# First stage of a hybrid backbone layer: fixed instruction order, squares paired and summed by TensorE, inverse norm multiplied in first

## Chip, cores and metric

The kernel runs on one NeuronCore of one Trainium2 chip. The metric is the time of the whole program on the device in microseconds; of several runs the median is given. All times inside a profile are microseconds from the first instruction of the profiled execution, unless they are marked ns.

## The reference, cut to what matters

One layer of a diffusion backbone over 1024 latent tokens and 256 context tokens, model width 1024. Both streams are normed, modulated (scale and shift made from a conditioning vector) and put through one wide projection; two recurrent branches, an output projection and a gated convolutional MLP follow.

```python
def rmsnorm(x, w):
    xf = x.astype(jnp.float32)
    y = xf * lax.rsqrt(jnp.mean(xf * xf, axis=-1, keepdims=True) + EPS)
    return (y * w.astype(jnp.float32)).astype(x.dtype)

def modulate(h, shift, scale):
    return h * (1 + scale) + shift
...
        mx = jnp.split((sc @ ada_w[l] + ada_b[l])[:, None, :], 6, axis=-1)
        mc = jnp.split((scc @ ada_w[l] + ada_b[l])[None, None, :], 6, axis=-1)
        hx = modulate(rmsnorm(x, norm_mix_w[l]), mx[0], mx[1])
        hc = modulate(rmsnorm(ctx, norm_mix_w[l]), mc[0], mc[1])
        oc, ox = mixer(hc, hx, w_in[l], ...
```

The change touches only the making of `hx` and `hc` and the first columns of the projection `h @ w_in`.

## The kernel before

Activations lie with the 1024 channels on partitions: eight tiles `xk[0..7]` of 128 channels x 1024 tokens for the latent stream, and `cx` (128 x 8 x 256) for the context. Every dense product is made in three passes on values split in two parts (`hi` = the value rounded to fp32r, `lo` = the rest): hi*hi, hi*lo, lo*hi. So each normed tile has a high and a low half (`xh[k]`, `xl[k]`, in the pool tiles H0 to H15; `ch[k]`, `cl[k]` for the context), and each weight tile a `whi` and a `wlo`, made by ScalarE and VectorE from the loaded `raw`.

`start()` is the first stage. SyncE's queue loads `xk`, `cx`, two groups of eight modulation weight tiles (`aw[0]` in H8 to H15, `aw[1]` in `adaw`), and the first weight tiles (`raw`: one for the step sizes, "dt", one for the recurrent input "lx", one for its gate "lg"). `norm_latent()` squares the eight `xk` on ScalarE and adds them up on VectorE into `ssx`; `token_rs()` sums over partitions by TensorE (line 199: a 128 x 128 block of the sums is the stationary operand, one column of ones the moving one; eight matmuls for 1024 tokens) and makes the inverse root (`rsqrt()`); `spread()` brings the result to all partitions (line 209: diagonal tiles `xdg` times ones, into PSUM), and ScalarE copies it to SBUF (`xrs`). `norm_context()` does the same for `cx`. `ada_group(q)` makes scale and shift (`sc`, `sv`) of four of the eight channel tiles: 32 matmuls at line 311, a copy `row`, two small matmuls at line 319, three VectorE instructions. Group 0 serves k = 0 to 3, group 1 serves k = 4 to 7.

Then a loop over k modulates one tile of each stream (`mod(k)`: value times scale times inverse norm on VectorE, `hi` with the shift on ScalarE, `lo` on VectorE) and hands four accumulations one step each (`gdense`, line 125): dt and lx over the context (`pre[0]`, `pre[1]`, 6 matmuls of 256 columns per k together), lx and lg over the latent tokens (`pre[2]`, `pre[3]`, 6 matmuls of 512 columns per k each). The last two lie in the pool `psD`, which has two buffers.

What order the instructions get on each engine is decided by the framework's scheduler: it may move an instruction ahead of others of its engine where the data allow it. `pin()` marks an instruction as kept in program order when `self.pinned` is set; before the change that is so only far later, in the MLP. Each engine, and SyncE's queue of transfers, works off its list strictly in that order.

Of the kernel before, what the change touches and what calls it, by code (L numbers as in the profile page):

```python
# [15 lines left out]
P = 128  # L16
# [29 lines left out]
class Builder:  # L46
# [31 lines left out]
    def wload(self, src, n=1024, kn=8):  # L78
        nc = self.nc
        with self.prio():  # L80
            raw = self.t(self.wp, n, "raw")
            nc.sync.dma_start(raw, src)
# [35 lines left out]
    def gdense(self, ps, w, xh, xl, spans, kn=8, xo=0):  # L118
        nc = self.nc
        hi, lo = w  # L120
        for k in range(kn):
            for i, (a, b) in enumerate(((hi, xh), (hi, xl), (lo, xh))):
                for (s, e) in spans:
                    o = ps[s // H] if isinstance(ps, list) else ps[:, s:e]
                    nc.tensor.matmul(o, a[:, k, :], b[k][:, xo + s : xo + e],  # L125
                                     start=(k == 0 and i == 0), stop=(k == kn - 1 and i == 2))
            yield
# [48 lines left out]
    def rsqrt(self, pool, ps, n, inv, tag):  # L176
# [5 lines left out]
        nc.vector.tensor_scalar(v, ps, inv, EPS, op0=ALU.mult, op1=ALU.add)  # L182
        self.act(a, v, AF.Sqrt)
        nc.vector.reciprocal(r, a)
        self.tt(a, r, r)
        self.tt(a, a, v)
        nc.vector.tensor_scalar(a, a, -0.5, 1.5, op0=ALU.mult, op1=ALU.add)
# [3 lines left out]
    def token_rs(self, pool, parts, n, inv, tag, ps=None):  # L191

        nc = self.nc
        nch = n // P
        if ps is None:
            ps = self.t(self.psS, nch, "s")
        for c in range(nch):
            for i, q in enumerate(parts):
                nc.tensor.matmul(ps[:, c : c + 1], q[:, c * P : (c + 1) * P], self.ones[:, 0:1],
                                 start=(i == 0), stop=(i == len(parts) - 1))  # L200
        return self.rsqrt(pool, ps[:, :nch], nch, inv, tag)

    def spread(self, pool, r, out, tag):

        nc = self.nc
        for c in range(r.shape[1]):
            dg = self.t(pool, P, tag + "dg")
            nc.vector.tensor_scalar(dg, self.ident, r[:, c : c + 1], None, op0=ALU.mult)
            nc.tensor.matmul(out[:, c * P : (c + 1) * P], self.ones, dg, start=True, stop=True)
# [61 lines left out]
    def setup(self, cpool):  # L271
# [14 lines left out]
        self.act(self.a_neg, self.v("a_log"), AF.Exp)  # L286
        nc.vector.tensor_scalar_mul(self.a_neg, self.a_neg, -1.0)
# [17 lines left out]
    def ada_group(self, pool, q, w, scc):  # L305
# [3 lines left out]
        for k in range(8):  # L309
            for g in range(4):  # L310
                nc.tensor.matmul(ps[32 * g : 32 * g + 32, :], scc[:, k, :], w[k][:, g * 256 : g * 256 + 256],
                                 start=(k == 0), stop=(k == 7))
# [5 lines left out]
        for i in range(2):  # L318
            nc.tensor.matmul(pt[:, i], row[:, i * P : (i + 1) * P], pick, start=True, stop=True)
# [32 lines left out]
    def start(self, cpool, ch, cl):  # L352
        nc, tc, A = self.nc, self.tc, self.A
        with tc.tile_pool(name="st1", bufs=1) as p1, tc.tile_pool(name="st2", bufs=2) as p2:
# [6 lines left out]
            for k in range(8):  # L361
                nc.sync.dma_start(aw[0][k], A["ada1"][0, k])
            scc = self.t(p1, [8, 32], "scc")
            nc.gpsimd.memset(scc, 0.0)
            self.lam_chain(cpool, p1)
            self.act(scc[:, :, 0:2], self.v("cc", n=16).rearrange("p (k i) -> p k i", i=2), AF.Silu)
            self.warm = self.t(cpool, 1, "warm")
            self.act(self.warm, self.ones[:, 0:1], AF.Sqrt)

            def norm_context():  # L370
                sq = [self.t(self.pH, [4, TX], f"H{h}") for h in range(2)]
                for h in range(2):
                    self.act(sq[h], cx[:, 4 * h : 4 * h + 4, :], AF.Square)
                self.tt(sq[0], sq[0], sq[1], op=ALU.add)
                self.tt(sq[0][:, 0:2], sq[0][:, 0:2], sq[0][:, 2:4], op=ALU.add)
                cr = self.token_rs(p1, [sq[0][:, 0], sq[0][:, 1]], TX, 1.0 / D, "cr")
                pcr = self.t(self.psS, TX, "s")
                self.spread(p2, cr, pcr, "x")
                crs = self.t(p1, TX, "ssc")
                self.act(crs, pcr, AF.Copy)  # L380
                return crs

            def norm_latent():
                ssx = self.t(p1, T, "ssx")
# [6 lines left out]
                pxr = [self.t(self.psS, H, "s") for _ in range(2)]  # L391
                xrs = self.t(p1, T, "ssx")
                for i in range(2):
                    self.spread(p2, xr[:, 4 * i : 4 * i + 4], pxr[i], "x")
                    self.act(xrs[:, i * H : i * H + H], pxr[i], AF.Copy)
                return xrs

            xrs = norm_latent()
            crs = norm_context()
            self.xh, self.xl = [], []  # L400

            def mod(k):
                self.modulate(cx[:, k, :], cx[:, k, :], crs, ch[k], cl[k], self.sc[:, k, 1:2], self.sv[:, k, 1:2])
# [4 lines left out]
            order = [("dt", -1), ("lx", M_LX), ("lg", M_LG)]  # L408
            self.wahead = 0
            ws = [self.take(key) for key in order[:2]]  # L410
            for k in range(8):
                nc.sync.dma_start(aw[1][k], A["ada1"][1, k])
            ws.append(self.take(order[2]))
            groups = [self.ada_group(p2, q, aw[q], scc) for q in range(2)]
            for _ in groups[0]:
                pass
            self.wahead = self.AHEAD[0]
            self.pre = [self.t(self.psS, TX, "s"), self.t(self.psS, TX, "s"),
                        self.t(self.psD, T, "d"), self.t(self.psD, T, "d")]
            X = [(0, TX)]  # L420
            gens = [self.gdense(self.pre[0], ws[0], ch, cl, X), self.gdense(self.pre[1], ws[1], ch, cl, X),
                    self.gdense(self.pre[2], ws[1], self.xh, self.xl, self.FULL),
                    self.gdense(self.pre[3], ws[2], self.xh, self.xl, self.FULL)]
# [1102 lines left out]
```

## Time and profile before

| | |
|---|---|
| median of 3 runs (lowest, highest) | 2298.85 us (2298.83, 2303.24) |
| the profiled execution's own time | 2300.16 us |
| its span, first to last instruction | 2298.4 us |
| TensorE busy | 2216.4 us, 96% |
| VectorE, ScalarE, GpSimd busy | 1627.4, 1178.3, 330.5 us |
| granted TensorE clock, mean over the span | 0.992 |
| last matmul of `start()` ends (line 125 on `pre[3]`) | 79.41 us |

The profiled execution's own time is 1.76 us more than its span, and 1.31 us above the median of the runs. A view called timeline lists instructions in order of time: start, length, engine, line, what it writes and reads, how many were merged (x4), and in brackets the idle time before it and what ended that. A view called windows gives each engine's busy time in a stretch. The profile shows a TensorE instruction as two records, PEld (load of the stationary operand) and PE (the matmul); a plain f32 matmul, as in the norms, is run as two such pairs.

### The profile page before, as it was taken

What the parts mean: (1) busy time and instruction counts of PE and PEld (TensorE: products, weight loads), DVE (VectorE), ACT (ScalarE), POOL (GpSimd) and SP (SyncE); (2) the same over time, 40 slices, a digit from 0 to 9 for tenths busy, and PEclk for the clock granted to TensorE, in tenths of its full rate; (3) what the DMA queues carried; (4) which work ended last, traced back from release to release, by engine and by line L of the source; (5) the groups of instructions that cost most, each with busy time, mean ns of one, the idle gap of its engine ahead of it and who ended that gap; (6) DMA issues with size and microseconds to landing.
All of it is one profiled execution on the core that took longest, in us unless ns stands there. A gap on an engine that the chain in (4) does not pass through costs nothing.

```text
span 2298.4 us, 29736 instructions
## 1 busy us (share of the span) xinstructions
PE 2216.4 (96%) x11302; PEld 1844.5 (80%) x11302; DVE 1627.4 (71%) x2554; ACT 1178.3 (51%) x1796; POOL 330.5 (14%) x255
## 2 busy tenths in 40 slices
PE   5999999999999999999999999999889999999998
PEld 3887888787888888888888778888668888878888
DVE  5789688889888858858866675457877777774335
ACT  4597888486666556656635322335334444442121
POOL 0000000000000000000000000001757777730000
PEclk9999999999999999999999999999999999999999
DMA  7222222243444434424348775532122222254212
GB/s 279 78 78 88 83 85 65 79 147 123 120 137 139 125 100 145 146 79 151 118 121 273 232 237 178 177 123 64 37 64 83 83 83 83 82 168 129 71 55 74
DMA packets 88943, 274.87 MB, mean 120 GB/s; under 512 B 10560, under 2 KB 16736, under 8 KB 84576
## 3 DMA queue, kind: packets, MB, share of 16 engines
q1 hardware_dynamic: 88800, 272.97, 37.2%
q8 instruction: 89, 1.46, 0.3%
q14 instruction: 54, 0.44, 0.1%
HBM read 233.85 MB, written 39.08 MB: 119 GB/s over the span
## 4 chain that ended last, share of the span: by engine, by line
PE 72%; DVE 11%; ACT 7%; DMA 6%; issue 3%; POOL 1%; SPq 0%; POOLq 0%; DVEq 0%; ACTq 0%
PE d L125 29%; PE s L125 17%; PE d L1173 11%; PE s L1173 5%; PE s L939 2%; ACT L L163 2%; ACT L163 2%; DMA adar<-in_ada 2%; PE s L931 1%; PE s L604 1%; DMA gk<-gd 1%; DVE wlo L160 1%; PE s L880 1%; DVE facc L157 1%; PE s L879 1%
## 5 line engine op out<-in xcount | busy, mean ns | idle before, releaser
L125 PE MATMUL d<-H,whi 128*128 128x512 f32 x2496 | 700.0, 398 | 2.9 <-ACT whi L163 1.6
L125 PEld LDWEIGHTS d<-H,whi 128*128 128x128 f32 x2496 | 456.4, 189 | 97.4 <-issue 5.6
L125 PE MATMUL d<-H,wlo 128*128 128x512 f32 x1248 | 392.3, 393 | 2.6 <-DVE wlo L160 2.6
L163 ACT ACTIVATE whi<-raw 128x1024 fp32r<-128x1024 f32 (+2 forms) x194 | 186.1, 960 | 290.1 <-PE s L125 117.1
L125 PEld LDWEIGHTS d<-H,wlo 128*128 128x128 f32 x1248 | 233.1, 188 | 52.5 <-DVE wlo L160 4.0
L157 DVE SCALAR_TENSOR_TENSOR facc<-d,vec,facc 128x945 f32<-128x945 f32 (+2 forms) x176 | 214.6, 1221 | 74.7 <-ACT facc L163 70.5
L160 DVE TENSOR_TENSOR wlo<-raw,whi 128x1024 fp32r<-128x1024 f32 (+1 forms) x154 | 188.0, 1222 | 76.8 <-ACT whi L163 70.1
L125 PE MATMUL s<-H,whi 128*128 128x512 f32 x672 | 202.6, 390 | 0.8 <-ACT whi L163 0.8
L163 ACT ACT_TABLE_LOAD x125 | 160.4, 1283 | 70.4 <-DVE bc L157 22.8
L1086 POOL TENSOR_TENSOR ssq<-H,A 128x512 f32<-128x512 f32 x4 | 6.0, 1501 | 1171.1 <-ACT H L163 1166.8
L125 PEld LDWEIGHTS s<-H,whi 128*128 128x128 f32 x672 | 125.7, 188 | 28.1 <-ACT whi L163 1.8
L125 PE MATMUL s<-A,whi 128*128 128x512 f32 x480 | 138.4, 390 | 1.1 <-POOL A L1086 1.0
L157 DVE SCALAR_TENSOR_TENSOR M<-s,mods,M 128x512 f32<-128x512 f32 (+1 forms) x72 | 49.5, 690 | 119.1 <-PE s L125 118.9
L125 PE MATMUL s<-H,wlo 128*128 128x512 f32 x336 | 126.0, 391 | 2.2 <-DVE wlo L160 2.1
L125 PEld LDWEIGHTS s<-A,whi 128*128 128x128 f32 x480 | 90.0, 188 | 20.6 <-POOL A L1086 1.4
L157 DVE SCALAR_TENSOR_TENSOR E<-E,cst 128x128 f32<-128x128 f32 x256 | 81.7, 350 | 22.6 <-ACT E L163 22.6
L160 DVE TENSOR_TENSOR L<-L,L 128x1280 f32<-128x1280 f32 (+3 forms) x50 | 69.7, 1401 | 38.8 <-ACT L L163 38.5
L163 ACT ACTIVATE m<-GU,dtt 128x128 f32<-128x128 f32 x256 | 79.1, 391 | 31.5 <-PE s L931 26.4
L1173 PE MATMUL d<-A,whi 128*128 128x512 f32 x372 | 91.6, 396 | 1.5 <-DVE facc L157 1.5
L157 DVE SCALAR_TENSOR_TENSOR m<-GL,dtt,m 128x128 f32<-128x128 f32 x256 | 78.2, 349 | 20.3 <-ACT m L163 20.3
L163 ACT ACTIVATE E<-E,cst 128x128 f32<-128x128 f32 x256 | 81.2, 393 | 21.0 <-DMA E<-csd 21.0
L1173 PE MATMUL d<-A,wlo 128*128 128x512 f32 x348 | 86.2, 398 | 5.2 <-ACT ssq L163 5.2
(333 smaller groups left out, 4250.3 us busy)
## 6 DMA issues: line engine op xcount, KB each, us to landing
raw<-in_w SPq DMA_DIRECT2D x92, 512.0 KB, 3.6
E<-csd SPq DMA_DIRECT2D x32, 1024.0 KB, 5.3
A<-in_wup SPq DMA_DIRECT2D x40, 512.0 KB, 4.2
R<-csd SPq DMA_DIRECT2D x64, 256.0 KB, 4.3
adar<-in_ada SPq DMA_DIRECT2D x32, 512.0 KB, 4.4
hd<-facc SPq DMA_DIRECT2D x22, 512.0 KB, 5.1
gated<-sg SPq DMA_DIRECT2D x32, 256.0 KB, 2.9
gd<-y SPq DMA_DIRECT2D x32, 256.0 KB, 3.6
```

What stands on the lines that cost most here:

```text
L125: nc.tensor.matmul(o, a[:, k, :], b[k][:, xo + s : xo + e], start=(k == 0 and i == 0), stop=(k == kn - 1 and i == 2))
L157: self.pin(self.nc.vector.scalar_tensor_tensor(out, in0, s, in1, op0=op0, op1=op1))
L160: return self.pin(self.nc.vector.tensor_tensor(out, a, b, op=op))
L163: return self.pin(self.nc.scalar.activation(out, in_, f, **kw))
L604: nc.tensor.matmul(pg, a[:, q, :], b[:, s:e], start=(i == 0), stop=(i == 2))
L879: nc.tensor.matmul(ps[:, s - s2, 0, :], btok[:, s, :], xw[:, 0, s, :], start=True, stop=True)
L880: nc.tensor.matmul(ps[:, s - s2, 1, :], btok[:, 7 - s, :], xw[:, 1, 7 - s, :], start=True, stop=True)
L931: nc.tensor.matmul(psy[q, c, :], self.xt[:, c0 + c, q], m[:, h, c, :], start=True, stop=True)
L939: nc.tensor.matmul(pso[:, c, :], S[:, cc if d == 0 else 7 - cc, d, :], CT[:, cc * P : (cc + 1) * P], start=True, stop=True)
L1086: self.pin(self.nc.gpsimd.tensor_tensor(out, a, b, op=op))
L1173: q = self.pin(self.nc.tensor.matmul(ps, a[:, k, :], b, start=(k == 0 and i == 0 and p in ("11", "12", "s3")), stop=(k == 3 and i == 2), s ...
```

## The change

It does five things, all inside `start()`:

- From the loads on, every instruction is pinned: each engine gets them in the order in which the code writes them.
- Squares are added in pairs (four VectorE adds instead of seven), and `token_sums()` lets TensorE add the four pair sums while it sums over partitions: 32 line-199 matmuls instead of eight.
- The inverse norm is not copied to SBUF. It stays in PSUM (`pxr`, one of `psD`'s two buffers) and is multiplied into `xk` and `cx` (`scaled(k)`, two halves per tile; two instructions for `cx`) ahead of scale and shift, which then need one ScalarE instruction per latent tile and one VectorE instruction per context tile; `hi` is a further ScalarE copy, `lo` a VectorE subtraction.
- `aw[1]` and the third weight tile (into H7) are asked for early in the code.
- Group 1 of the modulation is computed at k = 3 in one piece. The fourth accumulation starts after k = 5 and then makes up its first six steps at once, because its PSUM buffer is `pxr`'s until `scaled(7)`.

```diff
+            px = self.t(self.psS, 8, "s")
+            pairs = []
+            for k in range(KD):
+                sq = self.t(self.pH, T, f"H{k}" if k < 6 else "H6") if k != 7 else self.t(p1, T, "sq7")
+                self.act(sq, xk[k], AF.Square)
+                pairs.append(sq)
+                if k % 2:
+                    self.tt(pairs[k - 1], pairs[k - 1], sq, op=ALU.add)
...
-                for k in range(KD):
-                    s2 = ssx if k == 0 else self.t(p2, T, "modt")
-                    self.act(s2, xk[k], AF.Square)
-                    if k:
-                        self.tt(ssx, ssx, s2, op=ALU.add)
-                xr = self.token_rs(p1, [ssx], T, 1.0 / D, "xr")
...
+            self.token_sums(px, pairs[::2], 8)
+            xr = self.rsqrt(p1, px, 8, 1.0 / D, "xr")
+            self.tt(sq[0], sq[0], sq[1], op=ALU.add)
+            pxr = self.t(self.psD, T, "d")
+            self.spread(p2, xr, pxr, "x")
+            self.tt(sq[0][:, 0:2], sq[0][:, 0:2], sq[0][:, 2:4], op=ALU.add)
+            pc = self.t(self.psS, 2, "s")
+            self.token_sums(pc, [sq[0][:, 0], sq[0][:, 1]], 2)
+
+            def scaled(k):
+                for (s, e) in self.FULL:
+                    self.tt(xk[k][:, s:e], xk[k][:, s:e], pxr[:, s:e])
+
+            scaled(0)
+            cr = self.rsqrt(p1, pc, 2, 1.0 / D, "cr")
+            pcr = self.t(self.psS, TX, "s")
+            self.spread(p2, cr, pcr, "x")
+            scaled(1)
+            for h in range(2):
+                c = cx[:, 4 * h : 4 * h + 4, :]
+                self.tt(c, c, pcr.unsqueeze(1).to_broadcast([P, 4, TX]))
+            groups = [self.ada_group(p2, q, aw[q], scc) for q in range(2)]
+            next(groups[0])
+            next(groups[0])
...
+            def ctx(k):
+                self.pin(nc.vector.tensor_scalar(cx[:, k, :], cx[:, k, :], self.sc[:, k, 1:2], self.sv[:, k, 1:2],
+                                                 op0=ALU.mult, op1=ALU.add))
+                self.act(ch[k], cx[:, k, :], AF.Copy)
+
+            def latent(k):
                 self.xh.append(self.t(self.pH, T, f"H{2 * k}", F32R))
                 self.xl.append(self.t(self.pH, T, f"H{2 * k + 1}", F32R))
-                self.modulate(xk[k], xk[k], xrs, self.xh[k], self.xl[k], self.sc[:, k, 0:1], self.sv[:, k, 0:1])
+                self.act(xk[k], xk[k], AF.Identity, bias=self.sv[:, k, 0:1], scale=self.sc[:, k, 0:1])
+                self.act(self.xh[k], xk[k], AF.Copy)
+
+            def low(k):
+                self.tt(cl[k], cx[:, k, :], ch[k].bitcast(F32), op=ALU.subtract)
+                self.tt(self.xl[k], xk[k], self.xh[k].bitcast(F32), op=ALU.subtract)
...
             for k in range(KD):
-                mod(k)
-                if k in (1, 2):
-                    next(groups[1])
+                if k + 2 < KD:
+                    scaled(k + 2)
+                if k == 3:
+                    for _ in groups[1]:
+                        pass
+                if k + 1 < KD:
+                    ctx(k + 1)
+                    latent(k + 1)
+                low(k)
+                if k == 0:
+                    ws.append(self.wload(None, raw=raws[2]))
                 for g in gens:
                     next(g)
+                if k == 5:
+                    self.pre[3] = self.t(self.psD, T, "d")
+                    gens.append(self.gdense(self.pre[3], ws[2], self.xh, self.xl, self.FULL))
+                    for _ in range(6):
+                        next(gens[3])
+            self.pinned = False
+            self.wnext = 3
```

The other lines of the diff wrap existing instructions in `pin()`, give `wload` an already loaded `raw`, and split `token_sums` out of `token_rs`.

How the order on the engines moves is seen at three places. The first is TensorE's list at its very beginning, before: `ssx` holds the sum of all squares, and the eight matmuls of the latent sum stand as one row ahead of the spread and the context's sum.

```order
L199 MATMUL s_214<-ones_75,ssx_191 128x1 x8
L209 MATMUL s_233<-xdg_236,ones_75 128x128
L209 MATMUL s_233<-xdg_239,ones_75 128x128
L209 MATMUL s_233<-xdg_242,ones_75 128x128
L209 MATMUL s_233<-xdg_245,ones_75 128x128
```

Now, the last of eight token blocks and what follows it (H_66, H_68, H_70 and H_72 are the four pair sums):

```order
L204 MATMUL s_204<-ones_75,H_66_205 128x1
L204 MATMUL s_204<-ones_75,H_68_210 128x1
L204 MATMUL s_204<-ones_75,H_70_215 128x1
L204 MATMUL s_204<-ones_75,H_72_220 128x1
L213 MATMUL d_273<-xdg_274,ones_75 128x128
```

These four rows stand there eight times over, and since the first token block already needs the last pair sum, only three of the 32 matmuls stand ahead of the first one that does.

The second place is TensorE's list in the loop, before: `s_359` and `s_360` are the context accumulations, `d_361` the one of lx, `adaw` the weights of modulation group 1.

```order
L125 MATMUL s_359<-ch_12_97,whi_96_294 128x256
L125 MATMUL s_360<-ch_12_97,whi_99_300 128x256
L311 MATMUL s_397<-adaw_145,scc_161 32x256 x4
L125 MATMUL d_361<-H_111_366,whi_99_300 128x512 x2
L125 MATMUL s_359<-cl_20_105,whi_96_294 128x256
L125 MATMUL s_359<-ch_12_97,wlo_97_295 128x256
L125 MATMUL s_360<-cl_20_105,whi_99_300 128x256
L125 MATMUL s_360<-ch_12_97,wlo_100_301 128x256
L311 MATMUL s_397<-adaw_146,scc_161 32x256 x4
```

Now, around the end of k = 2 and the beginning of group 1 (`s_457`), with `d_374` the accumulation of lx:

```order
L126 MATMUL d_374<-H_111_415,whi_105_381 128x512 x2
L126 MATMUL d_374<-H_112_416,whi_105_381 128x512 x2
L126 MATMUL d_374<-H_111_415,wlo_106_382 128x512 x2
L313 MATMUL s_457<-adaw_143,scc_173 32x256 x4
L313 MATMUL s_457<-adaw_144,scc_173 32x256 x4
L313 MATMUL s_457<-adaw_145,scc_173 32x256 x4
L313 MATMUL s_457<-adaw_146,scc_173 32x256 x4
```

Group 1 stood between the first four steps of the loop, one weight tile at a time from the first step on; now all of it stands behind the third step's last matmul.

The third place is VectorE's list behind the scale and shift of group 0, before: the two `wlo` follow each other, and every `H` written is the low half of a latent tile.

```order
L160 TENSOR_TENSOR sv_79<-s_353,vec_72 128x8 x2
L157 SCALAR_TENSOR_TENSOR sc_80<-sv_79,vec_72 128x8
L157 SCALAR_TENSOR_TENSOR cx_119<-cx_119,sc_80,ssc_290 128x256
L157 SCALAR_TENSOR_TENSOR xk_29_120<-xk_29_120,sc_80,ssx_235 128x1024
L160 TENSOR_TENSOR wlo_97_295<-raw_292,whi_96_294 128x1024
L160 TENSOR_TENSOR wlo_100_301<-raw_298,whi_99_300 128x1024
L157 SCALAR_TENSOR_TENSOR cl_20_105<-cx_119,sv_79,ch_12_97 128x256
L157 SCALAR_TENSOR_TENSOR H_112_367<-xk_29_120,sv_79,H_111_366 128x1024
```

Now (`d_273` is `pxr`):

```order
L161 TENSOR_TENSOR sv_79<-s_362,vec_72 128x8 x2
L158 SCALAR_TENSOR_TENSOR sc_80<-sv_79,vec_72 128x8
L161 TENSOR_TENSOR wlo_99_369<-raw_159,whi_98_368 128x1024
L422 TENSOR_SCALAR cx_117<-cx_117,sc_80,sv_79 128x256
L161 TENSOR_TENSOR wlo_106_382<-raw_161,whi_105_381 128x1024
L161 TENSOR_TENSOR xk_31_120<-xk_31_120,d_273 128x512 x2
L422 TENSOR_SCALAR cx_117<-cx_117,sc_80,sv_79 128x256
L161 TENSOR_TENSOR cl_20_103<-cx_117,ch_12_95 128x256
L161 TENSOR_TENSOR H_104_378<-xk_29_118,H_103_377 128x1024
L161 TENSOR_TENSOR wlo_110_396<-H_55_163,whi_109_395 128x1024
```

The first `wlo` moved ahead of the context tile, the second one and `wlo_110` stand alone, each behind a `whi` that ScalarE makes after a whole latent tile. From the first matmul behind `start()` on, the lists of TensorE, VectorE and GpSimd are the same as before; on ScalarE and VectorE one split of a small weight tile (`gh`, `gl`) and in SyncE's queue one transfer (`gw`) stand earlier by a few places.

## Rows read from the trace of the kernel before

**Rows 1.** The page, its head and busy times of the whole span.
```profile
span 2298.4 us, 29736 instructions
...
PE 2216.4 (96%) x11302; PEld 1844.5 (80%) x11302; DVE 1627.4 (71%) x2554; ACT 1178.3 (51%) x1796; POOL 330.5 (14%) x255
```

**Rows 2.** Windows: stretch, length, PE, PEld, DVE, ACT, POOL busy, clock, DMA, GB/s.
```profile
17.90:40.80 22.90, 16.26 (x112) 12.67 (x112) 7.82 (x29) 5.78 (x11) 0.00 (x0) 1.00 0.96 381
40.80:79.40 38.60, 36.94 (x214) 26.43 (x215) 30.92 (x41) 17.92 (x23) 0.50 (x3) 0.96 0.18 53
79.40:260.00 180.60, 174.95 (x986) 151.13 (x985) 149.33 (x180) 149.23 (x184) 0.00 (x0) 1.00 0.27 84
```

**Rows 3.** Timeline of TensorE, 0 to 41 us.
```profile
17.92 3.55 PE L199 MATMUL s<-ones,ssx 128*128 128x1 f32 x16 [17.92 <-DVE ssx L160]
23.40 3.79 PE L209 MATMUL s<-xdg,ones 128*128 128x128 f32 x16 [1.94 <-DVE xdg L208]
27.72 1.87 PE L199 MATMUL s<-ones,H 128*128 128x1 f32 x8 [0.53 <-DVE H L160]
...
32.60 5.36 PE L311 MATMUL s<-H,scc 128*32 128x256 f32 x64
...
40.81 0.39 PE L125 MATMUL s<-ch,whi 128*128 128x256 f32 x1 [1.67 <-ACT ch L163]
```

**Rows 4.** Timeline of TensorE, 73 to 79.5 us.
```profile
73.04 1.09 PE L125 MATMUL d<-H,whi 128*128 128x512 f32 x4
...
75.78 0.28 PE L125 MATMUL s<-ch,whi 128*128 128x256 f32 x1
75.90 0.28 PE L125 MATMUL s<-cl,whi 128*128 128x256 f32 x1
...
78.79 0.62 PE L125 MATMUL d<-H,wlo 128*128 128x512 f32 x2
```

**Rows 5.** Timeline of SyncE's queue, 14 to 18 us (issues of transfers).
```profile
14.79 0.33 SPq L362 DMA_DIRECT2D H<-in_ada  x1
17.28 0.33 SPq L362 DMA_DIRECT2D H<-in_ada  x1
```

**Rows 6.** Groups by shape, 0 to 77 us: busy us, mean ns of one.
```profile
L163 ACT ACTIVATE H<-xk,sv 128x1024 fp32r<-128x1024 f32 x8 | 9.2, 1152 | 4.3 <-DVE xk L157 4.3
...
L163 ACT ACTIVATE whi<-raw 128x1024 fp32r<-128x1024 f32 x4 | 4.2, 1046 | 0.0
...
L157 DVE SCALAR_TENSOR_TENSOR cl<-cx,sv,ch 128x256 fp32r<-128x256 f32 x8 | 3.9, 485 | 0.0
```

**Rows 7.** Timeline of VectorE, 23 to 44 us.
```profile
23.06 0.88 DVE L208 TENSOR_SCALAR xdg<-ident,xrr 128x128 f32<-128x128 f32 x4
...
39.46 0.17 DVE L157 SCALAR_TENSOR_TENSOR sc<-sv,vec 128x8 f32<-128x8 f32 x1
...
41.40 2.36 DVE L160 TENSOR_TENSOR wlo<-raw,whi 128x1024 fp32r<-128x1024 f32 x2
```

**Rows 8.** Line 199 alone: ns min/median/max, first and last start in us.
```profile
L199 PE MATMUL s<-ones,ssx x16: 344/352/353, 17.9 to 21.1; 128*128 128x1 f32 x16
```

**Rows 9.** Timeline of TensorE at 644 us, the same instruction amid dense matmuls.
```profile
643.82 0.95 PE L199 MATMUL s<-ones,ssq 128*128 128x1 f32 x8
```

**Rows 10.** Groups by shape on VectorE, 76 to 260 us.
```profile
L214 DVE TENSOR_SCALAR L<-L 128x256 f32<-128x256 f32 x1 | 0.3, 295 | 0.5 <-ACT L L163 0.5
```

**Rows 11.** Instructions on the tile t: a 512-column product read from PSUM.
```profile
L160 DVE TENSOR_TENSOR t<-s,R x64: 681/691/694, 499.4 to 1193.9; 128x512 f32<-128x512 f32 x64
```

**Rows 12.** Instructions on adaw, group 1: ns min/median/max, first and last start.
```profile
L311 PE MATMUL s<-adaw,scc x64: 379/403/636, 42.1 to 56.0; 128*32 128x256 f32 x64
```

**Rows 13.** Windows: group 0's beginning, and a stretch early in the loop (columns as before).
```profile
32.60:35.90 3.30, 3.30 (x33) 1.58 (x36) 0.00 (x0) 0.39 (x1) 0.00 (x0) 1.00 1.02 408
42.80:46.20 3.40, 3.14 (x14) 1.55 (x14) 3.40 (x5) 0.43 (x1) 0.00 (x0) 0.52 0.70 200
```

**Rows 14.** The page's transfers: KB each, median us from issue to landing.
```profile
raw<-in_w SPq DMA_DIRECT2D x92, 512.0 KB, 3.6
```

More of the change, by code (lines that the diff above doesn't have):

```diff
@@ L124, in gdense @@
                     o = ps[s // H] if isinstance(ps, list) else ps[:, s:e]
-                    nc.tensor.matmul(o, a[:, k, :], b[k][:, xo + s : xo + e],
-                                     start=(k == 0 and i == 0), stop=(k == kn - 1 and i == 2))
+                    self.pin(nc.tensor.matmul(o, a[:, k, :], b[k][:, xo + s : xo + e],
+                                              start=(k == 0 and i == 0), stop=(k == kn - 1 and i == 2)))
             yield
@@ L207, in spread @@
             dg = self.t(pool, P, tag + "dg")
-            nc.vector.tensor_scalar(dg, self.ident, r[:, c : c + 1], None, op0=ALU.mult)
-            nc.tensor.matmul(out[:, c * P : (c + 1) * P], self.ones, dg, start=True, stop=True)
+            self.pin(nc.vector.tensor_scalar(dg, self.ident, r[:, c : c + 1], None, op0=ALU.mult))
+            self.pin(nc.tensor.matmul(out[:, c * P : (c + 1) * P], self.ones, dg, start=True, stop=True))
     def log1p01(self, e, d, s, q):
@@ L310, in ada_group @@
             for g in range(4):
-                nc.tensor.matmul(ps[32 * g : 32 * g + 32, :], scc[:, k, :], w[k][:, g * 256 : g * 256 + 256],
-                                 start=(k == 0), stop=(k == 7))
+                self.pin(nc.tensor.matmul(ps[32 * g : 32 * g + 32, :], scc[:, k, :], w[k][:, g * 256 : g * 256 + 256],
+                                          start=(k == 0), stop=(k == 7)))
         yield
@@ L318, in ada_group @@
         for i in range(2):
-            nc.tensor.matmul(pt[:, i], row[:, i * P : (i + 1) * P], pick, start=True, stop=True)
+            self.pin(nc.tensor.matmul(pt[:, i], row[:, i * P : (i + 1) * P], pick, start=True, stop=True))
         o = VOFF["ada_b"]
@@ L362, in start @@
                 nc.sync.dma_start(aw[0][k], A["ada1"][0, k])
+            order = [("dt", -1), ("lx", M_LX), ("lg", M_LG)]
+            raws = []
+            for i, (key, m) in enumerate(order):
+                raws.append(self.t(self.wp, T, "raw") if i < 2 else self.t(self.pH, T, "H7"))
+                nc.sync.dma_start(raws[i], A["wdt"] if key == "dt" else A["w1"][m])
+            for k in range(8):
+                nc.sync.dma_start(aw[1][k], A["ada1"][1, k])
             scc = self.t(p1, [8, 32], "scc")
@@ L364, in start @@
             nc.gpsimd.memset(scc, 0.0)
+            self.pinned = True
+            self.act(self.a_neg, self.v("a_log"), AF.Exp)
             self.lam_chain(cpool, p1)
+            self.pin(nc.vector.tensor_scalar_mul(self.a_neg, self.a_neg, -1.0))
             self.act(scc[:, :, 0:2], self.v("cc", n=16).rearrange("p (k i) -> p k i", i=2), AF.Silu)
             self.warm = self.t(cpool, 1, "warm")
-            self.act(self.warm, self.ones[:, 0:1], AF.Sqrt)
[L370 to L381, printed above, removed]
@@ new lines, in start @@
+            pc = self.t(self.psS, 2, "s")
[8 more added lines that the diff above has]
+            scaled(1)
+            for h in range(2):
+                c = cx[:, 4 * h : 4 * h + 4, :]
+                self.tt(c, c, pcr.unsqueeze(1).to_broadcast([P, 4, TX]))
@@ L404, in mod @@
                 self.xh.append(self.t(self.pH, T, f"H{2 * k}", F32R))
                 self.xl.append(self.t(self.pH, T, f"H{2 * k + 1}", F32R))
-                self.modulate(xk[k], xk[k], xrs, self.xh[k], self.xl[k], self.sc[:, k, 0:1], self.sv[:, k, 0:1])
[L408 to L419, printed above, removed]
+                self.act(xk[k], xk[k], AF.Identity, bias=self.sv[:, k, 0:1], scale=self.sc[:, k, 0:1])
+                self.act(self.xh[k], xk[k], AF.Copy)
```

47 lines of the change are left out of this document (21 added, 26 removed).

## Prediction

> **What bounds the kernel now.** I read the page first: TensorE is busy for 96% of a span of 2298.4 us [rows 1], so a microsecond counts only if TensorE gets it. Next the windows. In the stretch behind the first stage TensorE is busy for 174.95 of 180.6 us: it can absorb 5.65 us there at the very most. In the loop of the stage it works 36.94 of 38.6 us, but in the 22.9 us ahead of the loop only 16.26 [rows 2]. The third view is TensorE's timeline at the start [rows 3]. It shows one chain: the latent sums over partitions begin at 17.92 and take 3.55 us, the spread of the inverse norm ends at 27.19, the context's sums begin at 27.72, modulation group 0 runs from 32.60 to 37.96, and the loop's first matmul starts at 40.81. The stage's last matmul ends at 79.41 [rows 4]. Behind it TensorE's and VectorE's lists are as before, so what the stage gains or loses goes into the end nearly one to one. I follow the new chain to the new end of the stage.
>
> **Up to the latent sums.** SyncE's queue keeps eight transfers under way; the issue at 14.79 waits for `xk[7]`, the one at 17.28 for `cx` [rows 5]. The squaring of 1024 columns is a ScalarE instruction like those of 1046 ns, an add a VectorE one like the two `wlo` that took 2.36 together, so 1.22 alone and 1.14 behind another [rows 6, 7]. The last pair sum is there at 14.8 + 1.05 + 1.2 = 17.1. Before, the sums began at 17.92: 0.8 us are won.
>
> **The latent sums, the largest term.** Before, eight matmuls of one column are 16 records in 3.55 us, starts (21.1 - 17.9)/15 = 0.213 apart [rows 3, 8]. Now there are 32. Three fit in ahead of the last pair sum; the other 29 are 58 records, 12.4 us. The sums end at 29.6 instead of 21.47.
>
> Is 0.213 the right spacing? The granted-clock column reads 1.00 for this stretch [rows 2], but the same instruction amid dense matmuls takes eight records in 0.95 us, 0.119 each [rows 9], so I read the start as the lower of the two levels, 1.2 GHz. From 17.92 to 29.59 (sums, spread, sums) TensorE was busy for 9.2 of 11.7 us and the spacing stayed; I keep 0.213 for all 58 records, and 0.119, which is 5.5 us less, for the other end. The Trainium skill, "TensorE: Matmul & The Clock Gate", section "LDWEIGHTS (loading the stationary operand)", gives a load as columns divided by 1.2 in ns, 107 ns for 128 columns, however many columns follow. By it 58 loads would take an estimated 6.2 us and the total below would be 16 us instead of 22; the rows at the start contradict it by a factor of two.
>
> **From the sums to the loop.** The small root instructions take 21.47 to 23.06, 1.6 us [rows 3, 7]. Then, in program order, a 1024-column add for the context stands ahead of the diagonals: 1.1 us that lay beside TensorE's spread before. Diagonals and spread: 23.06 to 27.19, 4.1. Context sums to the end of its spread: 27.72 to 32.60, 4.9; `scaled(0)` lies beside them. Group 0: 5.4. Its copy, pick and scale: 37.96 to 39.63 (39.46 plus 0.17), 1.7 [rows 3, 7]. That is 29.6 + 1.6 + 1.1 + 4.1 + 4.9 + 5.4 + 1.7 = 48.4. A `wlo` now stands ahead of the context tile on VectorE (1.1); the context tile itself has no row, the nearest is 295 ns for a 256-column multiply-add with constants [rows 10], the dearest 485 [rows 6]; I take 0.3, and for ScalarE's copy 0.4, an estimate from its 1046 ns for 1024 columns. The loop's first matmul starts at 50.2, 9.4 later than before. The removed PSUM copies on ScalarE lay beside TensorE's spread but for the last 0.6; the sum above has no such copy.
>
> **The loop.** ScalarE, behind the context tile, makes `xk[0]` (1.15), its high half (1.05) and only then the lx weight's high half (1.05): 53.4. VectorE's next instruction, that weight's `wlo`, waits for it, and behind it queue `scaled(2)`, the context tile and both low halves. `wlo` 1.2, `scaled(2)` two halves. A product of 512 columns from PSUM takes 691 ns [rows 11], so 1.3 for both. Context tile 0.25, its low half 0.4 (0.485 with the shift [rows 6]), latent low half 1.2: 57.8. The same happens with the lg weight, whose high half ScalarE makes behind the second latent tile, at 59.8: `wlo` at 61.0, second low half 64.1. From there VectorE sets a pace of 1.25 + 0.25 + 0.35 + 1.15 = 3.0 per tile, the third low half is there at 67.1. TensorE has 2.1 us of work per tile in this part (6 matmuls of 0.12 and 6 of 0.23 [rows 4]), so it waits.
>
> Then group 1 as one block. TensorE finishes the third tile 1.4 later, 68.5, computes group 1 (5.4, as group 0), 73.9, and 1.7 later VectorE has the scale: 75.6. VectorE, and ScalarE behind it, had nothing to do since 68.4, where `scaled(5)` ends. Before, group 1 stood among the first loop steps, and its last matmul began at 56.0 [rows 12]. Fourth low half 75.6 + 0.3 + 0.35 + 1.15 = 77.4, fifth 80.4, sixth 83.4.
>
> From the sixth on TensorE is the bound. It finishes the sixth step at 86 (0.9 of matmuls at full clock, 2.6 allowed: it ran at the lower level, 0.52 granted, from 42.8 to 46.2, after mostly waiting since 37.96 [rows 13], and now waits more). Then comes what the change deferred: all 48 matmuls of lg, 48 x 0.229 = 11.0, and the rest of the last two tiles, 2 x 2.1 = 4.2. The stage ends at 101.2 against 79.41: +21.8.
>
> **What costs nothing, and its cover.** The last three transfers of group 1 stand in SyncE's queue behind a weight transfer that waits for the lx `wlo` (54.6). 512 KB take 1.25 us ((17.28 - 14.79)/2, `cx` being 1024 KB) and 3.6 to land alone [rows 5, 14], so four land by 62; TensorE wants them at 68.5. That is 6 us of cover; if gone, each further microsecond counts fully. The lg weight is asked for ahead of group 1's weights and wanted at 58.7. The first transfer behind the stage (`gw`) waits for the last low half, near 90, 11 us ahead of the stage's end.
>
> **Sum.** -0.8 + 8.9 (58 - 16 records) + 1.1 + 0.2 of differences in small steps makes the 9.4 up to the loop; the loop itself takes 51.0 instead of 38.6, +12.4. Together +21.8. On the profiled execution's own time of 2300.16 (span 2298.4, 1.76 around it) that is 2322.0; its span is 1.3 above what the median of the runs, 2298.85, would have, so for a median I forecast **2320.6**.
>
> **Bounds.** Group 0 ran 33 records in its first 3.3 us [rows 13] and the other 31 in 2.06, its level changing on the way: at the lower level throughout, a group would take some 6.8 us, at the upper 3.4 to 3.7. Down: 0.119 for the sums, -5.5; both groups fast, 2 x -1.7; no allowance at the third and sixth step, -0.5 and -1.7. Together 2309.5. Up: group 1 slow throughout, +1.4; lg beginning at the lower level for as long as the slow stretch in the trace, 3.4 us at half speed, +1.7; the context's PSUM product with a broadcast operand, which has no row, at twice the 1.2 us, +2.4. Together 2326.
>
> **Rivals.**
> - *The faster level from the sums on* (chance 0.17). 32 matmuls without a gap may bring TensorE to 2.4 GHz where eight did not. For it: group 0 did become fast on its way. Against it: the spacing that stayed up to 29.59. It gives 2309 (the lower bound) to 2315 (the sums alone). The load time of the Trainium skill's page, cited above, would land here too.
> - *Lower level for longer* (0.09): TensorE waits so often in the first five steps that lg starts slow and group 1 never gets fast: 2324 to 2326, with the context's product 2328.
> - *Not slower* (0.08). The place is the loop: TensorE's own work there is 27.7 (96 matmuls of 0.229, 48 of 0.12) plus 5.4 for group 1, some 33 us. If VectorE and ScalarE kept far enough ahead that TensorE never waited, the stage would end at 50.2 + 33 = 83.3, +3.9, or 2302.7; with the fast sums as well, 2297.2. It decides where the loop lasts at most 33.8 us from 50.2. Against it stand the two `wlo` behind ScalarE and group 1 as a block: 18 us of waits that no other TensorE work in the list fills, since lg stands last.
> - The forecast itself, 2316 to 2324: 0.66.
>
> **Numbers.** 0.2% of 2298.85 is 4.6 us, about what a measurement can tell from no change. Faster needs gains that no row shows: 0.03. Same 0.05, from the third rival. Slower 0.92. The range 2309 to 2326 leaves out the third rival and the tails of the first two.
>
> **What would show it.** In the changed profile: line 204 on the latent sums with 64 records and some 12 us from 17.1 to about 29.6; the loop's first 256-column matmul near 50; VectorE waiting for `whi` near 53 and 59; VectorE and ScalarE idle for some 7 us while TensorE runs group 1 near 70; lg's 48 matmuls in one block at the end; the stage's last matmul near 101; behind it the same waits as before. It is wrong if the sums take half, if TensorE finds lg or group 1 earlier than the list says, or if the second stage's waits shrink by more than 1 or 2 us.

## The result and the profile after

The changed kernel takes 2317.47 us (median of 5 runs, 2310.32 to 2321.76); the kernel before took 2298.83 beside it (5 runs, 2295.84 to 2303.24). The ratio is 1.0075, 95% interval 1.006 to 1.009: slower by about 0.75%, inside the predicted range and 3 us below the forecast. The profiled execution's own time is 2319.18, its span 2317.5, 19.1 more than before. Line numbers have moved: 199, 209, 125, 311, 319, 160 and 163 are now 204, 213, 126, 313, 321, 161 and 164.

The page's busy times and the windows of the changed kernel (columns as in [rows 2]), answering to [rows 1, 2]:

```profile
PE 2226.6 (96%) x11350; PEld 1859.8 (80%) x11350; DVE 1625.2 (70%) x2561; ACT 1182.1 (51%) x1800; POOL 331.1 (14%) x255
```

```profile
17.20:29.80 12.60, 12.54 (x58) 12.45 (x58) 0.03 (x1) 3.49 (x4) 0.00 (x0) 1.00 1.03 410
29.80:50.10 20.30, 12.64 (x97) 9.25 (x97) 12.78 (x35) 3.15 (x11) 0.00 (x0) 1.00 0.22 86
50.10:70.00 19.90, 11.81 (x44) 9.32 (x48) 12.62 (x19) 11.82 (x13) 0.00 (x0) 0.57 0.50 184
70.00:99.20 29.20, 26.52 (x178) 20.55 (x171) 15.19 (x26) 15.18 (x19) 0.50 (x3) 1.00 0.11 28
99.20:300.00 200.80, 195.39 (x1103) 169.03 (x1102) 167.23 (x204) 162.22 (x206) 0.00 (x0) 1.00 0.28 87
```

TensorE is no less busy over the span (96%), but in the loop's first 20 us it works only 11.81 of 19.90, at a granted clock of 0.57. Its timeline, answering to [rows 3, 4]:

```profile
17.20 12.54 PE L204 MATMUL s<-ones,H 128*128 128x1 f32 x58 [1.96 <-DVE H L161]
32.62 3.78 PE L213 MATMUL d<-xdg,ones 128*128 128x128 f32 x16 [2.88 <-DVE xdg L212]
36.19 1.71 PE L204 MATMUL s<-ones,H 128*128 128x1 f32 x8
...
40.85 5.59 PE L313 MATMUL s<-H,scc 128*32 128x256 f32 x64
...
50.07 0.38 PE L126 MATMUL s<-ch,whi 128*128 128x256 f32 x1 [2.44 <-ACT ch L164]
56.35 0.58 PE L126 MATMUL s<-cl,whi 128*128 128x256 f32 x1 [5.90 <-DVE cl L161]
...
69.72 3.66 PE L313 MATMUL s<-adaw,scc 128*32 128x256 f32 x64
...
83.96 1.07 PE L126 MATMUL d<-H,whi 128*128 128x512 f32 x4
...
98.58 0.62 PE L126 MATMUL d<-H,wlo 128*128 128x512 f32 x2
```

The sums end at 29.74 instead of 21.47, the loop starts at 50.07 instead of 40.81, and the stage ends at 98.58 + 0.62 = 99.20 instead of 79.41: 19.8 later. From there to the end of the span it is 2218.3 us, before 2219.0, so the stage holds the whole loss. VectorE's timeline in the same stretch shows what it waits for:

```profile
40.95 2.35 DVE L161 TENSOR_TENSOR cx<-cx,s 128x1024 f32<-128x1024 f32 x2
...
53.21 1.23 DVE L161 TENSOR_TENSOR wlo<-raw,whi 128x1024 fp32r<-128x1024 f32 x1 [3.65 <-ACT whi L164]
...
59.61 1.22 DVE L161 TENSOR_TENSOR wlo<-H,whi 128x1024 fp32r<-128x1024 f32 x1 [2.18 <-ACT whi L164]
...
74.53 0.24 DVE L161 TENSOR_TENSOR sv<-s,vec 128x8 f32<-128x8 f32 x2 [6.52 <-PE s L321]
```

Two waits for a weight's high half, 3.65 and 2.18, stand where [rows 7] has the two `wlo` back to back. The third wait, 6.52, is the one for group 1's shift; in the kernel before VectorE waited 1.80 for it:

```profile
57.61 0.24 DVE L160 TENSOR_TENSOR sv<-s,vec 128x8 f32<-128x8 f32 x2 [1.80 <-PE s L319]
```

### The profile page after: what moved, and what is told of

Its sections match the earlier page's. It is cut to its first block, busy times and chain, and to the rows that moved or that the text cites. A ratio compares the mean times of both kernels' runs of the same rounds, so it can differ in the third digit from the quotient of the medians.

```text
span 2317.5 us, 29827 instructions
## 1 busy us (share of the span) xinstructions
PE 2226.6 (96%) x11350; PEld 1859.8 (80%) x11350; DVE 1625.2 (70%) x2561; ACT 1182.1 (51%) x1800; POOL 331.1 (14%) x255
## 4 chain that ended last, share of the span: by engine, by line
PE 74%; DVE 11%; ACT 6%; DMA 5%; issue 2%; POOL 1%; SPq 0%; POOLq 0%; DVEq 0%; ACTq 0%
PE d L126 29%; PE s L126 18%; PE d L1207 11%; PE s L1207 5%; PE s L973 3%; ACT L L164 2%; DMA adar<-in_ada 2%; ACT L164 2%; PE s L965 1%; DMA gk<-gd 1%; PE s L638 1%; PE s L914 1%; PE s L913 1%; DVE wlo L161 1%; DVE facc L158 1%
```

## The experiments

My theory after this trace had four costs: the 32 sums, the two serial weight splits, group 1 as one block, and lg behind it. The rivals were that one of them covers the others, that the clock level and not the count makes the sums dear, that the fixed order alone is to blame, or the product by the inverse norm. The stage's end is what I read; the runs' times are a check on it, since the rest of the program takes 2214.8 to 2219.0 us in all traces but one. Each stage's end is that of one execution.

**Sums by VectorE (e1).** VectorE adds the pair sums up, TensorE sums one tile:

```diff
                 if k % 2:
                     self.tt(pairs[k - 1], pairs[k - 1], sq, op=ALU.add)
+                if k in (3, 5, 7):
+                    self.tt(pairs[0], pairs[0], pairs[k - 1], op=ALU.add)
...
-            self.token_sums(px, pairs[::2], 8)
+            self.token_sums(px, pairs[:1], 8)
```

> The change with VectorE adding the four pair sums into one tile, so that TensorE again sums over partitions with 8 one-column matmuls instead of 32. Theory (the 32 matmuls at 0.213 us a record cost 8.9 of the 19.8 us by which the stage is longer): the last add stands 1.1 to 1.2 us behind the old last pair sum, at 18.3; 16 records take 3.4 to 3.6, the sums end near 21.9 instead of 29.74, the stage's last matmul near 91.3 instead of 99.20, and the time is 7 to 8 us below the changed kernel's 2317.5, some 2309.5. Rival (the loop's order fixes the end, the sums are hidden): if VectorE's and ScalarE's lists in the loop or the arrival of the modulation weights set the end, the sums end early but less than 3 us of it reach the stage's end, 2314 to 2318.

Measured: 2306.27 us, ratio to the kernel before 1.004 (1.0025 to 1.0055). TensorE's timeline:

```profile
18.67 3.54 PE L204 MATMUL s<-ones,H 128*128 128x1 f32 x16 [18.67 <-DVE H L161]
...
28.59 0.95 PE L204 MATMUL s<-ones,H 128*128 128x1 f32 x8
...
32.77 4.90 PE L313 MATMUL s<-H,scc 128*32 128x256 f32 x64
...
41.31 0.39 PE L126 MATMUL s<-ch,whi 128*128 128x256 f32 x1 [2.45 <-ACT ch L164]
...
88.08 0.62 PE L126 MATMUL d<-H,wlo 128*128 128x512 f32 x2
```

The stage ends at 88.70, 10.5 earlier, more than the 8 expected. The sums end 7.5 earlier; 1.2 more come up to the loop, above all from the context's sums (0.95 instead of 1.71) and group 0 (4.90 instead of 5.59); the stretch from the loop's start to group 1 is 1.7 shorter, at a granted clock of 0.71:

```profile
41.30:59.20 17.90, 9.28 (x36) 6.71 (x36) 12.56 (x19) 11.81 (x13) 0.00 (x0) 0.71 0.58 205
```

So the long row of one-column matmuls costs its own length, 7.5. The other 2.9 go with more of TensorE's work at the upper level, and this trace does not show that the row is their cause. For the 1.2 ahead of the loop e2 speaks against it: it keeps the row of 32 and has nearly the same short context's sums and group 0.

**Group 1 early (e2).** Its matmuls go to k = 1, the rest of it one step on:

```diff
-                if k == 3:
-                    for _ in groups[1]:
-                        pass
+                if k == 1:
+                    next(groups[1])
...
                 low(k)
+                if k == 2:
+                    next(groups[1])
```

> The change with modulation group 1 split: its 64 matmuls behind the second tile's low halves' place in the list (k = 1), its copy, pick and scale one step later, where the kernel before has them, instead of all of it as one block at k = 3. Theory (the block costs what VectorE waits for it): the wait of 6.5 us in front of group 1's shift shrinks to less than 2; the weights of group 1 land by about 62, which allows that; the stage ends 4 to 6 us earlier, at 93 to 95, near 2312.5. Rival (the time is only moved: TensorE owes the 48 matmuls of lg behind anyway, and VectorE's pace of 3.0 a tile is the floor): the wait goes but the stage's end moves by less than 2 us, 2315.5 to 2317.5.

Measured: 2312.2 us, ratio 1.0063 (1.005 to 1.0076); the stage ends at 93.55, 5.65 earlier, as expected. VectorE's wait for group 1's shift falls from 6.52 to 2.18:

```profile
67.82 0.24 DVE L161 TENSOR_TENSOR sv<-s,vec 128x8 f32<-128x8 f32 x2 [2.18 <-PE s L321]
```

Not all of the 5.65 is the edit's. Up to the loop the code is that of the changed kernel, yet the loop starts at 48.90 instead of 50.07, since the context's sums and group 0 take 1.4 less:

```profile
36.19 0.95 PE L204 MATMUL s<-ones,H 128*128 128x1 f32 x8
...
40.33 4.94 PE L313 MATMUL s<-H,scc 128*32 128x256 f32 x64
...
48.90 0.39 PE L126 MATMUL s<-ch,whi 128*128 128x256 f32 x1 [2.44 <-ACT ch L164]
```

About 4.5 us remain for the split of group 1. In the other traces too, a difference of some 1 us between two stage ends can come from when TensorE's level rises.

**Lg in the loop (e3).** The inverse norm goes to SBUF, which frees its PSUM buffer for lg from the first step on:

```diff
+            xrs = self.t(p1, T, "sq7")
+            for (s, e) in self.FULL:
+                self.act(xrs[:, s:e], pxr[:, s:e], AF.Copy)
             def scaled(k):
-                for (s, e) in self.FULL:
-                    self.tt(xk[k][:, s:e], xk[k][:, s:e], pxr[:, s:e])
+                self.tt(xk[k], xk[k], xrs)
...
+                    gens.append(self.gdense(self.pre[3], ws[2], self.xh, self.xl, self.FULL))
```

(the last line stands at k = 0; the block at k = 5 is gone.)

> The change with the inverse norm copied from PSUM to a tile in SBUF by ScalarE, so that its PSUM buffer is free and the 48 matmuls of lg run within the loop, six at each tile, as before the change; the products of the latents read SBUF and have 1024 columns. Theory (TensorE waits for VectorE in the first five steps, so lg's matmuls fill time in which it is idle): the block of 48 at the end (11 us) goes, the stage ends 4 to 10 us earlier, at 89 to 95; 2308 to 2313. Rival (SBUF products of 1.22 in place of two PSUM halves, and the copies of 2 us on ScalarE ahead of the context, cost what lg gives; the stage's end is set by VectorE): less than 3 us, 2314.5 to 2317.5.

Measured: 2315.72 us, ratio 1.0078 (1.0065 to 1.0092), not to be told from the changed kernel. In the trace the stage ends at 95.72, 3.5 earlier. My expectation was too high. VectorE's wait for group 1's shift stays, and the group still starts at 70.62, behind three steps; only the lg matmuls of those three steps moved into idle time (18 x 0.229 = 4.1), and the loop started 0.9 later.

```profile
75.44 0.24 DVE L161 TENSOR_TENSOR sv<-s,vec 128x8 f32<-128x8 f32 x2 [6.77 <-PE s L321]
```

**Weights split early (e4).** All three weight splits go ahead of the modulation groups:

```diff
+            ws = [self.wload(None, raw=r) for r in raws]
             groups = [self.ada_group(p2, q, aw[q], scc) for q in range(2)]
...
-            ws = [self.wload(None, raw=raws[0])]
...
-            ws.append(self.wload(None, raw=raws[1]))
...
-                if k == 0:
-                    ws.append(self.wload(None, raw=raws[2]))
```

> The change with the three weight tiles split into high and low halves ahead of the modulation groups, where ScalarE and VectorE wait for TensorE, instead of within the loop's first steps. Theory (two low halves of the weights wait for ScalarE, 3.65 and 2.18 us, and one stands ahead of the first context tile): the waits go, VectorE saves three adds of 1.1 to 1.2 in the loop, the first loop matmul starts about 1 us earlier and the stage ends 6 to 9 us earlier, at 90 to 93; 2308.5 to 2311.5. Rival (TensorE has work to catch up, and group 1 as one block waits for its weights instead): the waits move to group 1 and less than 3 us are won, 2314.5 to 2317.5.

Measured: 2304.81 us, ratio 1.0034 (1.0021 to 1.0048); the stage ends at 89.50, 9.7 earlier. The two waits are gone, and all 9.7 are won by group 1's start:

```profile
50.83 0.38 PE L126 MATMUL s<-cl,whi 128*128 128x256 f32 x1 [1.01 <-DVE cl L161]
...
60.02 3.66 PE L313 MATMUL s<-adaw,scc 128*32 128x256 f32 x64
```

The waits (3.65 + 2.18) and three adds of 1.14 on VectorE make 9.2, which I should have added up beforehand.

**No fixed order (e5).** The changed code, ordered by the scheduler:

```diff
-            self.pinned = True
+            self.pinned = False
```

> The change without its fixed order: the same instructions, the scheduler orders the first stage again. By its lists the weights' splits then stand ahead of the modulation groups, the products of the latents run ahead, and group 1's matmuls are strewn among the first tiles; the 32 sums stay. Theory (order in the loop and number of sums are two separate costs): the sums still take 12.5 us and end at 29.7, the loop's waits mostly go, the stage ends 8 to 12 us earlier than 99.2, and the time is 2305 to 2309, still above 2298.85. Rival (the fixed order alone was the cause): within 2 us of the kernel before, 2297 to 2301.

Measured: 2306.53 us, ratio 1.004 (1.0026 to 1.0054); the stage ends at 88.42, 10.8 earlier, with the sums as long as ever:

```profile
17.21 12.53 PE L204 MATMUL s<-ones,H 128*128 128x1 f32 x58 [1.97 <-DVE H L161]
```

The fixed order, as it was written, is more than half of the loss, and not all of it.

**TensorE kept busy ahead of the sums (e6).** Added matmuls into a tile that nothing reads:

```diff
+            wps = self.t(self.psS, H, "s")
+            for _ in range(10):
+                self.pin(nc.tensor.matmul(wps[:, 0:P], self.ones, self.ones, start=True, stop=True))
...
                 self.act(sq, xk[k], AF.Square)
+                self.pin(nc.tensor.matmul(wps, self.ones, xk[k][:, 0:H], start=True, stop=True))
+                self.pin(nc.tensor.matmul(wps[:, 0:P], self.ones, self.ones, start=True, stop=True))
```

> The change with needless matmuls ahead of the latent sums: ten of ones with ones from 1 us on, then one of 512 and one of 128 columns as each latent tile arrives, into a PSUM tile that nothing reads; so TensorE comes to the sums working, not idle. Theory as predicted (the spacing of 0.213 us is that of the lower of TensorE's two levels): the records of the sums stand 0.119 apart, the 58 take 6.9 us instead of 12.54, they end near 24.1, and the stage ends about 5.5 us earlier; 2312. Rival (0.213 is what a one-column float32 matmul takes at this place whatever went before, as the level falls again or was not the cause): the sums' spacing stays at 0.21 and the time at 2316 to 2320.

Measured: 2314.2 us, ratio 1.008 (1.006 to 1.01), not to be told from the changed kernel; the stage ends at 96.28, 2.9 earlier. TensorE's timeline and windows (columns as in [rows 2]):

```profile
1.07 4.02 PE L384 MATMUL s<-ones 128*128 128x128 f32 x20 [1.07 <-POOL ones L282]
...
16.62 0.73 PE L204 MATMUL s<-ones,H 128*128 128x1 f32 x6
17.79 9.32 PE L204 MATMUL s<-ones,H 128*128 128x1 f32 x58 [0.44 <-DVE H L161]
```

```profile
17.60:21.00 3.40, 3.21 (x29) 3.21 (x29) 0.13 (x1) 3.01 (x3) 0.00 (x0) 1.00 1.03 410
...
22.00:27.20 5.20, 5.11 (x24) 5.02 (x24) 0.06 (x1) 0.00 (x0) 0.00 (x0) 0.50 1.03 408
```

Neither reading holds alone. The 58 records take 9.32, neither 6.9 nor 12.54: 32 of them start 0.112 apart, then 26 are 0.213 apart, and the granted clock reads 1.00 and then 0.50. So 0.213 is the spacing at the lower level, as the prediction read it. But the upper level did not last: with TensorE busy for 5.11 of 5.20 us, on one-column matmuls alone, it stood at 1.2 GHz.

**The four edits together (e7).** Edits e1 to e4 in one kernel; the fixed order and the product stay.

> The first four edits together (one tile of sums, group 1 among the first steps, lg in the loop, the weights' halves ahead of the modulation groups), with the fixed order and the product by the inverse norm kept. Theory (these four are the whole loss): the first loop matmul starts near 41, the stage ends at 76 to 81, and the time is 2294 to 2300, within 0.2% of 2298.85. Rival (the product ahead of scale and shift, an extra pass over the latents on VectorE, costs by itself): VectorE's pace of about 3 us a tile lasts, the stage ends at 84 or later, 2303 or more.

Measured: 2294.56 us, ratio 0.9988 (0.9978 to 0.9999). The loop starts at 42.57 and the stage ends at 78.04, 1.4 ahead of the kernel before. In the loop TensorE is busy for 34.50 of 35.6 us:

```profile
42.50:78.10 35.60, 34.50 (x214) 27.43 (x215) 23.95 (x36) 24.45 (x30) 0.50 (x3) 0.95 0.29 107
```

The four edits alone won 10.5, 5.65, 3.5 and 9.7, 29.3 together; jointly they win 21.2. They fill partly the same waits. With the order still fixed and the product kept, the loss is gone: it lay in what stood where in the order, and in the 32 sums, not in fixing an order as such.

**The sums alone in the kernel before (e8).** Only pairs and 32 matmuls, ordered by the scheduler:

```diff
-                    if k:
-                        self.tt(ssx, ssx, s2, op=ALU.add)
-                xr = self.token_rs(p1, [ssx], T, 1.0 / D, "xr")
+                    pairs.append(s2)
+                    if k % 2:
+                        self.tt(pairs[k - 1], pairs[k - 1], s2, op=ALU.add)
+                xr = self.token_rs(p1, pairs[::2], T, 1.0 / D, "xr")
```

> The kernel before with only the squares summed in pairs and 32 one-column matmuls over partitions. Theory (each of the 24 matmuls more costs two records of 0.213 us on the chain, 0.8 us come back from VectorE's shorter adds): the sums take 12.4 from 17.1 instead of 3.55 from 17.92, the stage ends 8 us later, near 87.5, and the time is 2306 to 2308. Rival (the scheduler hides them: the context's norm goes ahead of the latent's): less than 3 us, 2299 to 2302.

Measured: 2303.73 us, ratio 1.0033 (1.0021 to 1.0045); the stage ends at 86.78, 7.4 later than in the kernel before (8 expected; the time lies below the 2306 to 2308 expected). Nothing hides the sums, and the 0.8 us that VectorE's shorter adds were to give back did not come, since the 58 records start at 17.98 (17.92 before):

```profile
17.98 12.53 PE L199 MATMUL s<-ones,H 128*128 128x1 f32 x58 [1.97 <-DVE H L160]
```

**Product alone (e10).** The sums of e1 and the scheduler's order of e5. What remains of the change is the product ahead of scale and shift, with the PSUM buffer that its norm holds and the earlier requests for weights.

> The change without its fixed order and with 8 instead of 32 one-column matmuls: what is left of the change is the product by the inverse norm ahead of scale and shift. Theory (the three parts add up: sums 7.4, fixed order 10.8, product 1.6): the stage ends at 80 to 82, 1 to 2 us behind the kernel before, and the time is 2298 to 2301. Rival (the fixed order and the sums overlap, or the product costs more where the sums don't cover it): the stage ends at 84 or later, 2303 or more.

Measured: 2296.28 us, ratio 0.9996 (0.9984 to 1.0007): no change. The stage ends at 78.53, 0.9 ahead of the kernel before, against 80 to 82 expected. On balance the product costs nothing. It is not free on its way: group 0 is faster here (3.66 instead of 5.36), but behind it TensorE waits 5.11 for ScalarE ahead of the loop's first matmul (1.67 before), and the loop is then 36.7 long instead of 38.6. How much of this balance the faster group 0 pays for is not shown.

```profile
18.72 3.54 PE L204 MATMUL s<-ones,H 128*128 128x1 f32 x16 [18.72 <-DVE H L161]
...
31.84 3.66 PE L313 MATMUL s<-H,scc 128*32 128x256 f32 x64
...
41.79 0.80 PE L126 MATMUL d<-H,whi 128*128 128x512 f32 x1 [5.11 <-ACT H L164]
```

**Norms first (e9).** In e7 the loop is full, so the chain ahead of it is what is left. The squares are summed one by one again, and the context's sums and root move into the latents' waits; the first two products by the norm (`scaled(0)`, `scaled(1)`) move behind the weight splits:

```diff
-                if k % 2:
-                    self.tt(pairs[k - 1], pairs[k - 1], sq, op=ALU.add)
-                if k in (3, 5, 7):
-                    self.tt(pairs[0], pairs[0], pairs[k - 1], op=ALU.add)
+                if k:
+                    self.tt(pairs[0], pairs[0], sq, op=ALU.add)
...
+            self.token_sums(pc, [sq[0][:, 0], sq[0][:, 1]], 2)
             xr = self.rsqrt(p1, px, 8, 1.0 / D, "xr")
             pxr = self.t(self.psD, T, "d")
             self.spread(p2, xr, pxr, "x")
+            cr = self.rsqrt(p1, pc, 2, 1.0 / D, "cr")
+            pcr = self.t(self.psS, TX, "s")
+            self.spread(p2, cr, pcr, "x")
```

> The four edits together, and three more in the chain ahead of the loop: the squares are again summed one by one as the latent tiles arrive (last sum near 17.9 instead of 19.36), the context's squares are summed and its eight matmuls over partitions run in the wait for the latents' root, and the context's root and spread stand directly behind the latents' spread, so that group 0 follows as soon as its weights are there. Theory (with the loop full, what is left is the chain ahead of it: 1.4 from the sums, 1.1 from the add ahead of the diagonals, 3 from the context's norm): the loop's first matmul starts near 37 instead of 42.57, the stage ends 4 to 6 us earlier, at 72 to 74, and the time is 2289 to 2292, below the kernel before. Rival (VectorE is then late with the weights' low halves and group 1's weights land late, or the loop begins at the lower clock level): the first matmul starts early but the stage ends at 76 or later, 2293 to 2296.

Measured: 2286.03 us, ratio 0.9953 (0.9937 to 0.9969), faster than both kernels. TensorE's timeline:

```profile
17.91 3.55 PE L204 MATMUL s<-ones,H 128*128 128x1 f32 x16 [17.91 <-DVE H L161]
21.73 1.87 PE L204 MATMUL s<-ones,H 128*128 128x1 f32 x8 [0.27 <-DVE H L161]
23.50 3.78 PE L213 MATMUL d<-xdg,ones 128*128 128x128 f32 x16
...
28.29 3.66 PE L313 MATMUL s<-H,scc 128*32 128x256 f32 x64
...
36.59 0.58 PE L126 MATMUL s<-ch,whi 128*128 128x256 f32 x1 [2.77 <-ACT ch L164]
```

The loop starts 6.0 earlier than in e7 and the stage ends at 73.57, 4.5 earlier, as expected. The time fell by 8.5, but the intervals of the two ratios allow any fall from 2 to 14. The rest of the program took 2209.0 us in this trace, 6 less than in e7's, with the same code behind the stage; that part is not explained.

## Why the prediction was right, and where it was off

Two paths from one kernel to the other split the 19.8 us of the stage.

| path | stage's end, us |
|---|---|
| before, product (e10), fixed order (e1), 32 sums (the change) | 79.41, 78.53, 88.70, 99.20 |
| before, 32 sums (e8), product (e5), fixed order (the change) | 79.41, 86.78, 88.42, 99.20 |

The sums cost 7.4 to 10.5 (of the 10.5 the row itself is 7.5), the fixed order 10.2 to 10.8, and the rest, called the product here, -0.9 to +1.6.

**Up to the loop: right.** The last pair sum was there at 17.14 (predicted 17.1), the sums ended at 29.74 (29.6), the loop began at 50.07 (50.2). The spacing stayed 0.213, and e6 shows that this is the lower level. That the loop's start came within 0.1 is partly luck: e2, with the same code up to there, has it at 48.90. By the Trainium skill, "TensorE: Matmul & The Clock Gate", section "LDWEIGHTS (loading the stationary operand)", a load takes its columns divided by 1.2 in ns, an estimated 107 ns for 128 columns and 6.2 us for the 58 records. That is not borne out at the lower level, where the records stand 0.213 apart; at the upper level, in e6, they stand 0.112 apart, close to it.

**The two weight splits: right.** The high half of lx was there at 53.18 (53.4), the third low half at 66.82 (67.1). e4 shows that these waits with the adds were the dearest part of the order, 9.7.

**Group 1 as a block: right in kind, dear by 1.7.** VectorE idled 6.5 us there ("some 7"). The group took 3.66 us, not the 5.4 of group 0 that I put in: it ran at the upper level throughout, which I had only as a lower bound. TensorE began it 1.2 later than forecast, since it did the steps ahead of it largely at the lower level (0.57 granted), so 0.5 of the 1.7 reached the fourth low half (76.89 against 77.4).

**The sixth step: mis-sized.** I let it end at 86, with "2.6 allowed" for a slow clock behind waiting. It ended at 83.96, where lg's first matmul starts: the granted clock is 1.00 from 70 us on. From there the 48 lg matmuls and the last two tiles took 15.24 us against 15.2. These 0.5 and 1.5 are the 2.0 by which the stage's end was off (99.20, predicted 101.2). The rest of the 3 us between forecast and median is the end of the span, 0.7 nearer, and the scatter of the runs.

**The rivals.** The faster level from the sums on did not come, and e6 shows that even a running start holds it for only 32 of the 58 records. The lower level for longer was half there (0.57 in the loop's first 20 us, 0.71 with e1's short sums), but gone by group 1. "Not slower" was to decide where the loop lasts at most 33.8 us; it lasted 49.1. In e7 it lasts 35.5 from an earlier start, 42.57, and that kernel is indeed not slower.

## What to carry to other kernels

A fixed order must be written with each engine's queue in view: a weight split that needs two engines, put between a step's instructions, made VectorE wait twice and delayed every tile behind it, while the same split ahead of a stretch in which both engines wait for TensorE cost nothing (e4: the loop began 0.6 earlier, not later). Letting TensorE do a sum over tiles as well is no free addition when the operand is one column wide: each f32 matmul paid two loads of 128 columns, 2 x 0.213 us, on the chain, where VectorE's add of 1024 columns took 1.22 us beside the arriving data. When several edits fill the same wait, price them jointly: alone they won 29.3 us, together 21.2.

## What the runs showed of the hardware

- TensorE can be busy without pause and still be granted the lower clock: in e6, 0.50 in a stretch where one-column f32 matmuls filled 5.11 of 5.20 us, after 1.00 behind wider matmuls.
- At the start of these traces the spacing tells TensorE's level, the granted-clock column does not: in the changed kernel it reads 1.00 for 17.2 to 29.8 us, where the records stand 0.213 apart, as in the 0.50 stretch of e6, and not 0.112 apart, as in its 1.00 stretch. In e6 itself the 20 records from 1.07 us on stand first 0.213 and then 0.112 apart, under a reading of 1.00 throughout.
- The level need not rise at the same place in two executions of the same instructions: the changed kernel and e2 have the same code up to the loop, yet the context's sums took 1.71 and 0.95 us and group 0 took 5.59 and 4.94.
- A VectorE product of a 1024-column tile with a PSUM row broadcast over four channel tiles of the context, which had no row before, took 1.2 us, no dearer than a plain one (two of them 2.35).
